# Moving the forget-gate columns of an encoder layer into seven-product form, and token-major work beside the recurrence heads

## The chip, the cores and the metric

One core of a Trainium2 chip runs the whole program. The metric is the device time of one launch in microseconds (us), a median of several runs. TensorE (PE in the profile) multiplies matrices, VectorE (DVE), ScalarE (ACT) and GpSimd (POOL) work elementwise, and SyncE (SP) issues every DMA of this kernel from one queue, in order. Each engine executes its own list of instructions in the order that was fixed when the program was built.

## The reference

One encoder layer with 1024 positions and 1024 channels, in float32. The parts that matter here:

```
h = rms_norm(x);  z = h @ W_in          # q | f_fwd | f_bwd | i | out-gate | u | v | gate_a | gate_b
f = lb + (1-lb)*sigmoid(zf);  k = (1-lb)*sigmoid(-zf)       # forget gates and keys, two directions
o = scan_forward(q, k_f, v, f_f) + scan_backward(q, k_b, v, f_b)   # 8 heads of 128
A = rms_norm(o) * silu(zg)
u = gelu(zu);  v = layer_norm(gelu(zv))                      # the gated branch, 512 channels each
sg[g] = w_s[g] @ v[chunk, g] + b_s[g]                        # per chunk of 128 positions and group of 64
B = u * sg
mix = (sigmoid(gate_a)*(A @ W_a) + sigmoid(gate_b)*(B @ W_b)) @ W_out
x = x + rms_norm(mix);  x = x + rms_norm(SwiGLU(rms_norm(x)))
```

## The kernel before

**Products.** A float32 operand is split into a high and a low part (`split_into`, L114 on ScalarE and L115 on VectorE), and a product is three passes of matmuls (`mm3`, L133): 24 matmuls of 512 columns for one 128 x 512 block over 1024 channels. `Seven` (its matmuls are L278) computes a 2 x 2 block product with seven products of 12 matmuls in place of eight, so 84 matmuls where `mm3` takes 96. Its weight sums cost VectorE and ScalarE extra work.

**Stages.** After the start come the token-major groups (`tm_group`: positions on the partitions, 8 tiles x 24 matmuls each): the branch's v, the first half of the values i, the branch's u, the second half of the values. Between them lie the 8 spatial gating matmuls (L450), the transposes of B, and B @ W_b (`branch_b`: 8 column blocks x 2 x 12 matmuls). Then come 14 jobs of `Seven` for the columns gate_b, half of gate_a, the output gate zg and q; each result goes to DRAM (`m0_d`, `sig_d`, `zg_d`, `q_d`), and gate_b is multiplied there with B @ W_b.

**Heads.** `scores(h)` first multiplies q with keys (L613, operands `q,ks`), and then goes through seven levels (m = 1, 2, ... 64). A level is two groups of four 128 x 128 matmuls `ps_sc<-QA,X` (L624); VectorE updates `QA` (L633) and `X` (L636) for the next level, merges the result into `SC` (L646 copy_predicated up to m = 16, ScalarE L643 above), GpSimd makes `Y` (L660), VectorE halves `F` (L666). So every level waits for VectorE's update from the level ahead of it. `outputs(h)` transposes keys (L683), forms states (`S`: matmuls L688, VectorE L694), sums the output (`ps_o`, L712), normalises it on ScalarE (L715, L719; the root on GpSimd L101), transposes it (`ps_tr<-ident,on`, L722), and writes it to `at_d` (`on`, L724). In the program's order `proj` of head h+1 stands between `scores(h)` and `outputs(h)`: it computes the forward and the backward gate columns of one head, 2 x 2 x 24 = 96 matmuls `ps_mm<-hT..,whl` by `mm3`. In the last head `gate_a(0)` and `gate_a(1)` compute the other four blocks of gate_a, 8 x 24 matmuls. These matmuls, which no level waits for, are called fill below. After the heads come `merge` (A @ W_a, `ps_mm<-A,whl`), the output projection and the feed-forward part.

**Order.** The program is written under `tile.TileContext(nc, schedule_with_timeline_sim=True)`: the builder decides where each engine's instructions stand; tiles in pools (`bufs`) set what has to be free first.

Of the kernel before, what the change touches and what calls it, by code (L numbers as in the profile page):

```python
# [9 lines left out]
F32 = mybir.dt.float32  # L10
F32R = mybir.dt.float32r
# [11 lines left out]
H = 8  # L23
# [12 lines left out]
def kernel(ctx: ExitStack, tc: tile.TileContext, a: dict, out: bass.AP):  # L36
# [42 lines left out]
    v_d = dram.tile([H, P, NT, P], F32, name="v_d")  # L79
    m0_d = dram.tile([KD, P, T], F32, name="m0_d")  # L80
# [3 lines left out]
    bw_d = dram.tile([KD, P, T], F32, name="bw_d")  # L84
# [288 lines left out]
    def ev_i(half):  # L373
        def f(t, ps):
            s = t2(p0v, "vs", 4)
# [5 lines left out]
    def ev_u(t, ps):  # L381
        nc.scalar.activation(u[:, t], ps, AF.Gelu)

    def load_tm(gi, kk):
        pool = p0w if (4 * gi + kk) % 6 < 4 else whlp
        return load_split(a["w_tm"][gi, kk], [2, NH], nc.gpsimd if kk % 2 else nc.vector, pool, rawp)
# [26 lines left out]
    w = [load_tm(0, 0), load_tm(0, 1)]  # L413
# [3 lines left out]
    w += [load_tm(0, 2), load_tm(0, 3)]  # L417
# [5 lines left out]
    vn, u = [sgu.tile([P, NT, SGW], F32, name=name, tag="uv", bufs=2) for name in ("vn", "u")]  # L423
# [11 lines left out]
    w = [load_tm(1, kk) for kk in range(4)]  # L435
# [5 lines left out]
    close(c_x)  # L441
    tm_group(w, ev_i(0), layer_norm)
    close(c_t)
    w = [load_tm(2, kk) for kk in range(4)]
    tm_group(w, ev_u)
    for g in range(SGG):
        ps = ps_any()
        es = slice(g * SGE, (g + 1) * SGE)
        pv = ps.rearrange("p (c e) -> p c e", e=SGE)
        nc.tensor.matmul(pv, lhsT=wst[:, g, :], rhs=vn[:, :, es], start=True, stop=True)  # L450
        nc.vector.scalar_tensor_tensor(out=u[:, :, es], in0=pv, scalar=sgb[:, g:g + 1], in1=u[:, :, es],
                                       op0=ALU.add, op1=ALU.mult)
    c_b, p1b = phase("p1b", side="right")
    bT = [pair(p1b, f"bT{n}", None) for n in range(2)]
    for t in range(NT):
        tp = ps_tile(("tr", "o")[t % 2])
        for i in range(4):
            nc.tensor.transpose(tp[:, i * P:(i + 1) * P], u[:, t, i * P:(i + 1) * P], ident)
        ts = slice(t % 4 * P, (t % 4 + 1) * P)
        split_into(bT[t // 4][0][:, :, ts], bT[t // 4][1][:, :, ts], tp.rearrange("p (k t) -> p k t", k=4))  # L460
    w = [load_tm(3, kk) for kk in range(4)]
    tm_group(w, ev_i(1))
    close(c_w, c_v)

# [8 lines left out]
    def branch_b(j):  # L473
        raw = rawp.tile([P, KD, P], F32, name="raw", tag="raw")
        nc.sync.dma_start(raw[:, 0:4], a["w_b"][j])
        wb = whlp.tile([P, 2, KD, P], F32R, name="whl", tag="whl")[:, :, 0:4]
        split_into(wb[:, 0], wb[:, 1], raw[:, 0:4])
        for n in range(2):
            ps = ps_any()
            mm3(ps, lambda p, k: wb[:, p, k, :], lambda p, k: bT[n][p][:, k, :], 4)  # L480
            s = t2(p1t, "o", 2)
            nc.scalar.activation(s, ps, AF.Copy)
            nc.sync.dma_start(bw_d[j, :, n * NH:(n + 1) * NH], s)

    branch_b(0)
    branch_b(1)
# [10 lines left out]
    for k in range(4):  # L497
# [11 lines left out]
    for j in range(2, KD):  # L509
        branch_b(j)  # L510
    close(c_b)
# [36 lines left out]
    close(c_e, c_w, c_r, c_t, c_T)  # L548
# [3 lines left out]
    c_t, t1 = phase("s1t", 2)  # L552

# [7 lines left out]
    def proj(s, h, kinds):  # L561

        for kind in kinds:
            if kind == "q":
                s.q = hg.tile([P, T], F32, name="q", bufs=2)
                nc.sync.dma_start(s.q, q_d[h])  # L570
# [523 lines left out]
```

## Time and profile before

| what | value |
|---|---|
| median of 3 runs | 1968.68 us (1968.6 to 1969.14) |
| the profiled execution's own time | 1966.99 us |
| its span in the trace | 1965.2 us |
| mean granted TensorE clock | 0.997 |
| PE busy | 1910.8 us, 97% of the span |
| DVE busy | 1120.0 us, 57% |
| ACT busy | 757.2 us, 39% |
| POOL busy | 206.7 us, 11% |

The span is 1.8 us shorter than the execution's own time, which lies 1.7 us under the median. A stage is read from the row of its window: how long it is, and how much of it each engine was busy.

### The profile page before, as it was taken

To read this page: it belongs to the slowest core of one execution; us is meant where nothing else is said; L and a number is where in the kernel's file an instruction comes from. 1 tells how busy PE (TensorE), PEld (TensorE's weight loads), DVE (VectorE), ACT (ScalarE), POOL (GpSimd) and SP (SyncE) were. 2 spreads that over 40 slices of the span, in tenths; PEclk is the share of its full clock that TensorE was granted. 3 is DMA by queue.
4 is the path that set the end of the run, shared out by engine and by line. 5 is a ranking of instruction groups with operands and counts; after the bars stand their busy time and mean duration, and the time that the engine had idled before them with its cause. 6 is when DMAs were issued, how large, how long until landed. Compare 5 with 4: busy or idle time off the path is not lost.

```text
span 1965.2 us, 24005 instructions
## 1 busy us (share of the span) xinstructions
PE 1910.8 (97%) x9264; PEld 1596.0 (81%) x9264; DVE 1120.0 (57%) x1712; ACT 757.2 (39%) x1424; POOL 206.7 (11%) x153
## 2 busy tenths in 40 slices
PE   7999999999999999999989998999999999999999
PEld 6887888888887888888877887888888888888887
DVE  7402385544348777777665468855554537545743
ACT  6312254343354545545441356433333324112321
POOL 2600000000012222222112100000000000001000
PEclk9999999999999999999999999999999999999999
DMA  7220245323231221212336333232222106315222
GB/s 292 93 88 27 87 172 170 130 105 110 86 123 33 70 71 63 66 55 68 126 106 208 107 99 103 97 112 78 89 76 86 65 33 209 108 65 163 92 102 79
DMA packets 82690, 201.86 MB, mean 103 GB/s; under 512 B 8720, under 2 KB 18064, under 8 KB 82576
## 3 DMA queue, kind: packets, MB, share of 16 engines
q1 hardware_dynamic: 82576, 200.33, 30.2%
q8 instruction: 73, 1.20, 0.3%
q14 instruction: 41, 0.34, 0.0%
HBM read 147.35 MB, written 52.95 MB: 102 GB/s over the span
## 4 chain that ended last, share of the span: by engine, by line
PE 90%; DVE 4%; ACT 2%; DMA 2%; POOL 1%; issue 1%; SPq 0%; DVEq 0%; POOLq 0%; ACTq 0%
PE ps_mm L133 29%; PE ps_mm L278 20%; PE ps_sc L133 11%; PE ps_sc L278 10%; PE ps_st L133 6%; PE ps_sc L624 4%; PE ps_o L278 2%; PE ps_o L712 2%; PE ps_tr L278 2%; PE ps_st L278 1%; DVE QA L633 1%; POOL Y L660 1%; PE ps_st L688 1%; ACT SC L643 0%; DMA raw<-in_w_gate_dram 0%
## 5 line engine op out<-in xcount | busy, mean ns | idle before, releaser
L278 PE MATMUL ps_mm<-T,w 128*128 128x512 f32 x1296 | 309.6, 389 | 0.0
L278 PEld LDWEIGHTS ps_mm<-T,w 128*128 128x128 f32 x1296 | 243.2, 188 | 50.7 <-ACT u L228 0.2
L115 DVE TENSOR_TENSOR whl<-raw,whl 128x1024 fp32r<-128x1024 f32 (+1 forms) x70 | 89.6, 1282 | 142.7 <-ACT whl L114 142.6
L660 POOL TENSOR_TENSOR Y<-X,F 128x512 f32<-128x512 f32 x56 | 92.4, 1651 | 696.1 <-DVE F L599 392.4
L624 PE MATMUL ps_sc<-QA,X 128*128 128x128 f32 x896 | 126.4, 288 | 16.9 <-DVE QA L633 16.9
L115 DVE TENSOR_TENSOR w<-sums,w 128x1024 fp32r<-128x1024 f32 x72 | 88.0, 1223 | 94.2 <-ACT w L114 94.2
L624 PEld LDWEIGHTS ps_sc<-QA,X 128*128 128x128 f32 x896 | 116.1, 192 | 26.1 <-DVE QA L633 19.0
L133 PE MATMUL ps_mm<-whl,act 128*128 128x512 f32 x528 | 134.1, 389 | 0.0
L114 ACT ACTIVATE whl<-raw 128x1024 fp32r<-128x1024 f32 (+1 forms) x78 | 79.1, 1017 | 120.2 <-PE ps_sc L133 52.4
L633 DVE TENSOR_TENSOR QA<-QA,F 128x512 f32<-128x512 f32 x112 | 91.8, 828 | 49.2 <-PE ps_sc L624 48.1
L133 PE MATMUL ps_mm<-hTb,whl 128*128 128x512 f32 x480 | 118.6, 396 | 0.0
L133 PEld LDWEIGHTS ps_mm<-whl,act 128*128 128x128 f32 x528 | 99.1, 188 | 20.7
L133 PE MATMUL ps_mm<-hTa,whl 128*128 128x512 f32 x480 | 115.1, 392 | 0.0
L114 ACT ACTIVATE w<-sums 128x1024 fp32r<-128x1024 f32 x72 | 75.9, 1055 | 99.9 <-PE ps_sc L278 76.9
L278 PE MATMUL ps_sc<-T,w 128*128 128x512 f32 x432 | 107.5, 389 | 0.0
L133 PEld LDWEIGHTS ps_mm<-hTa,whl 128*128 128x128 f32 x480 | 89.4, 188 | 18.1
L133 PEld LDWEIGHTS ps_mm<-hTb,whl 128*128 128x128 f32 x480 | 88.2, 188 | 16.8
L278 PEld LDWEIGHTS ps_sc<-T,w 128*128 128x128 f32 x432 | 81.1, 188 | 16.9
L133 PE MATMUL ps_sc<-whl,act 128*128 128x512 f32 x354 | 91.0, 390 | 0.3 <-ACT acc L953 0.3
L133 PEld LDWEIGHTS ps_sc<-whl,act 128*128 128x128 f32 x354 | 66.3, 188 | 14.3 <-ACT acc L953 0.7
L115 POOL TENSOR_TENSOR wpg<-raw,wpg 128x1024 fp32r<-128x1024 f32 x4 | 9.6, 2403 | 598.3 <-ACT wpg L114 593.6
L278 PE MATMUL ps_mm<-B,wA 128*128 128x512 f32 x264 | 67.3, 399 | 1.7 <-ACT wA L114 1.7
(309 smaller groups left out, 3574.2 us busy)
## 6 DMA issues: line engine op xcount, KB each, us to landing
raw<-in_w_fm_dram SPq DMA_DIRECT2D x52, 512.0 KB, 3.6
raw<-in_w_gate_dram SPq DMA_DIRECT2D x22, 512.0 KB, 3.4
raw<-in_w_up_dram SPq DMA_DIRECT2D x22, 512.0 KB, 3.9
act_d<-s SPq DMA_DIRECT2D x22, 512.0 KB, 2.8
raw<-in_w_down_dram SPq DMA_DIRECT2D x22, 512.0 KB, 4.4
raw<-act_d SPq DMA_DIRECT2D x22, 512.0 KB, 4.2
raw<-in_w_tm_dram SPq DMA_DIRECT2D x16, 512.0 KB, 4.1
pr_d<-vs SPq DMA_DIRECT2D x16, 256.0 KB, 5.9
```

What stands on the lines that cost most here:

```text
L114: nc.scalar.activation(hi, src, AF.Copy)
L115: (eng or nc.vector).tensor_tensor(out=lo, in0=src, in1=hi.bitcast(F32), op=ALU.subtract)
L133: nc.tensor.matmul(ps, lhsT=lhs(lp, k), rhs=rhs(rp, k), start=(i == 0), stop=(i == n - 1))
L278: nc.tensor.matmul(ps, lhsT=lhs(lp, k), rhs=rhs(rp, k), start=(first and i == 0), stop=(i == n - 1), skip_group_check=True)
L624: nc.tensor.matmul(sp[:, i * P:(i + 1) * P], lhsT=X[:, c * P:(c + 1) * P], rhs=view(QA, c * P, [[2 * m, cb], [T + m, 2], [1, m]]), start=T ...
L633: nc.vector.tensor_tensor(out=view(QA, o, qd), in0=view(QA, o, qd), in1=view(F, of + 1, [[nb - 1, 2], [2, nb // 4], [0, m]]), op=ALU.mult)
L660: nc.gpsimd.tensor_tensor(out=view(Y, m, mid), in0=view(X, m, mid), in1=view(F, 0, [[4, nb // 4], [nb + 3, 2], [0, m]]), op=ALU.mult)
L688: nc.tensor.matmul(up[:, i * P:(i + 1) * P], lhsT=kt[:, i], rhs=v[:, c], start=True, stop=True)
L712: nc.tensor.matmul(op[:, i * P:(i + 1) * P], lhsT=l, rhs=r, start=(j == 0), stop=(j == len(terms) - 1))
```

## The change

1. `proj` is gone from the heads. The forget gates and keys of head h become a job ("fb", h) of `Seven`, with the forward columns as one block and the backward columns as the other. Eight such jobs stand among the column jobs (22 instead of 14). `gates` evaluates them and writes `F`, `X` and `Y` to DRAM (`f_d`, `xk_d`, `yk_d`); `load_head` reads them back ahead of each head. The temporaries `o` get 4 buffers instead of 2.
2. Three stages that stood ahead of the columns now stand beside the heads, where `proj` was: the second half of the values (heads 0 and 1), the gated branch u times `sg_d`, written to `ub_d` (heads 2 and 3), its transposes and B @ W_b (heads 4 and 5). gate_b is only written (`gb_d`) in the columns and multiplied in `branch_b`.
3. gate_a(0) moves to head 6, gate_a(1) stays in head 7. The finished heads' outputs are read back (`load_A`, `split_A`) there, two heads at a time. `v`, `zg`, `q` and `X` have one buffer each instead of two, and `load_values` stands behind `outputs` of the head before.
4. The T operands of `Seven` (`sums`) are made beside the second token-major group, and the layer norm of v inside the first.

```
-    tm_group(w, ev_u)
     for g in range(SGG):
         nc.tensor.matmul(pv, lhsT=wst[:, g, :], rhs=vn[:, :, es], start=True, stop=True)
-        nc.vector.scalar_tensor_tensor(out=u[:, :, es], in0=pv, scalar=sgb[:, g:g + 1], in1=u[:, :, es],
+        nc.scalar.activation(vn[:, :, es], pv, AF.Identity, bias=sgb[:, g:g + 1])
+    for t in range(NT // 2):
+        nc.sync.dma_start(sg_d[t], vn[:, 2 * t:2 * t + 2])
...
-    tm_group(w, ev_i(1))
...
-    branch_b(0)
-    branch_b(1)
...
-    for j in range(2, KD):
-        branch_b(j)
...
+    def gates(h, blocks):
+        for n in range(2):
+            ns = slice(n * NH, (n + 1) * NH)
+            keys = [t2(p1t, "o", 4) for _ in range(2)]
+            for d in range(2):
+                c = blocks[2 * d + n]
+                om = oml[:, d, h:h + 1]
+                cv = c.rearrange("p (t h) -> p t h", h=2)
+                for par in range(2):
+                    k = keys[par != d].rearrange("p (t h) -> p t h", h=2)[:, :, par]
+                    nc.scalar.activation(k, cv[:, :, par], AF.Sigmoid, scale=-1.0)
+                    nc.vector.tensor_scalar(out=k, in0=k, scalar1=om, scalar2=None, op0=ALU.mult)
+                Fd = t2(p1t, "o", 4) if 2 * d + n == 2 else c
+                nc.scalar.activation(Fd, c, AF.Sigmoid)
+                nc.vector.tensor_scalar(out=Fd, in0=Fd, scalar1=om, scalar2=lbt[:, d, h:h + 1], op0=ALU.mult, op1=ALU.add)
+                nc.vector.tensor_scalar(out=Fd, in0=Fd, scalar1=TINY, scalar2=None, op0=ALU.max)
+                nc.sync.dma_start(f_d[h, :, 1 - d, ns], Fd)
+            for k, k_d in zip(keys, (xk_d, yk_d)):
+                nc.sync.dma_start(k_d[h, :, ns], k)
...
-    jobs = [(kind, j) for kind, n in (("gb", KD), ("ga", NGA), ("zg", H), ("q", H)) for j in range(0, n, 2)]
+    jobs = [(kind, j) for kind, n in (("gb", KD), ("ga", NGA)) for j in range(0, n, 2)]
+    jobs = [job for h in range(6) for job in (("fb", h), jobs[h])] + [("fb", 6), ("fb", 7)]
+    jobs += [(kind, j) for kind in ("q", "zg") for j in range(0, H, 2)]
...
-            w = load_split(a["w_fm"][{"f": 8, "b": 16}[kind] + h], [KD, P], None, whlp, rawp)
-            for n in range(2):
-                mm3(ps, lambda p, k: w[:, p, k, :], fm_rhs(hT[n]), KD)
...
+    def load_head(s, h):
+        s.F = hg.tile([P, 2, T], F32, name="F")
+        nc.sync.dma_start(s.F, f_d[h])
...
-            proj(nxt, h + 1, "qfbg")
-        if h == H - 1:
+            load_head(nxt, h + 1)
+        if h < 2:
+            values(range(4 * h, 4 * h + 4))
...
+        elif h < 4:
+            branch(range(4 * (h - 2), 4 * (h - 1)))
+        elif h == 4:
+            bT = [pair(tmw, f"bT{n}", "tmw") for n in range(2)]
+            transpose_b(bT)
+            branch_b(bT, (0,))
+        elif h == 5:
+            branch_b(bT, (2, 4, 6))
+        elif h == 6:
             gate_a(0)
             A0 = new_fm("A0")
-            load_A(0, A0, range(H - 1), 5)
+            load_A(range(6))
+            for i in range(3):
+                split_A(0, A0, i)
+        else:
+            load_A([6])
             gate_a(1)
             A1 = new_fm("A1")
+            split_A(0, A0, 3)
...
         outputs(h, cur)
+        if h + 1 < H:
+            load_values(nxt, h + 1)
```

Three places show how the instructions moved. The first is TensorE's list (PE) in the middle of a late head, around the output sums of the head before (`ps_o`). Before, this piece of head 5 reads:

```order
2281 L712 MATMUL ps_o<-S,QA 128x128
2282 L624 MATMUL ps_sc<-QA,X 128x128 x2
2283 L133 MATMUL ps_mm<-hTb_150,whl 128x512
2284 L133 MATMUL ps_mm<-hTb_152,whl 128x512
2285 L133 MATMUL ps_mm<-hTb_150,whl 128x512
2286 L133 MATMUL ps_mm<-hTa_145,whl 128x512
2287 L133 MATMUL ps_mm<-hTa_147,whl 128x512
```

In the changed kernel the last four heads read like this (`A` is the normed output of earlier heads, `kt` transposed keys, `st` the state's sum):

```order
2509 L603 MATMUL ps_sc<-QA,X 128x128 x4
2510 L667 MATMUL ps_st<-v,kt 128x128 x3
2511 L603 MATMUL ps_sc<-QA,X 128x128 x12
2512 L667 MATMUL ps_st<-v,kt 128x128 x3
2513 L603 MATMUL ps_sc<-QA,X 128x128 x8
2514 L691 MATMUL ps_o<-S,QA 128x128
```

Where 24 or more fill matmuls stood between two levels, the levels now follow each other with only the short matmuls of `outputs` between them. The rows of the list say how the fill is spread. Before, 115 fill matmuls stand ahead of head 0's `q,ks` (counted from the last matmul of the columns), and between the `q,ks` of one head and the next 128, 96, 96, 96, 96, 96 and 143. In the changed kernel 79 stand ahead of head 0's, and then 213, 110, 153, 161, 43, 12 and 0 between them.

The second place is TensorE's list behind the last level of the last head (`X`, `Y` and `kt` are keys, `ps_st` the states' sums). Before, the transposes of both halves of head 6's outputs (rows 2709 and 2726) stand ahead of head 7's last levels:

```order
2726 L722 MATMUL ps_tr<-ident,on 128x128 x4
2727 L624 MATMUL ps_sc<-QA,X 128x128 x8
2728 L133 MATMUL ps_mm<-A_7479,whl 128x512 x2
2729 L133 MATMUL ps_mm<-A_7481,whl 128x512
2730 L133 MATMUL ps_mm<-A_7479,whl 128x512
2731 L133 MATMUL ps_mm<-A_7481,whl 128x512
2732 L133 MATMUL ps_mm<-A_7479,whl 128x512
2733 L624 MATMUL ps_sc<-QA,X 128x128 x8
```

In the changed kernel the last level of head 7 is row 2613, and behind it both halves of head 6's outputs follow (`ps_o`, and their transposes in rows 2626 and 2635), and then, as the last matmuls ahead of head 7's own outputs:

```order
2649 L667 MATMUL ps_st<-v,kt 128x128 x3
2650 L138 MATMUL ps_mm<-A_7353,whl 128x512 x2
2651 L138 MATMUL ps_mm<-A_7355,whl 128x512
2652 L138 MATMUL ps_mm<-A_7353,whl 128x512
2653 L138 MATMUL ps_mm<-A_7355,whl 128x512
2654 L138 MATMUL ps_mm<-A_7353,whl 128x512
2655 L667 MATMUL ps_sc<-v,kt 128x128 x3
2656 L691 MATMUL ps_sc<-v,SC 128x128
```

Rows 2650 to 2654 are six matmuls of `merge` that read the part of A in which head 6 lies, so they need its outputs written, read back and split. 42 matmuls `ps_sc<-A,whl` of `merge` (rows 2671 to 2703) stand in two parts of 21 ahead of the two transposes of head 7's outputs (rows 2687 and 2704), where before both transposes stand in one row with no matmul of `merge` between them.

The third place is VectorE's list (DVE) inside the column jobs. Before, it holds the sums, splits and adds of `Seven` there, and in the gate_b jobs four products with B @ W_b:

```order
302 L266 TENSOR_TENSOR p_3203<-ps_mm,p_3203 128x512
303 L268 TENSOR_TENSOR u_3217<-ps_sc,u_3217 128x512
304 L115 TENSOR_TENSOR w_3410<-sums,w_3410 128x1024
305 L203 TENSOR_TENSOR sums<-raw_3427 128x512
306 L204 TENSOR_TENSOR sums<-sums,raw_3422 128x512
```

In the changed kernel the gate arithmetic of a job of the new kind stands among them (`o`, `u` and `p` hold keys and gates, `oml` and `lbt` the bounds):

```order
187 L531 TENSOR_SCALAR o<-o,oml 128x256 x2
188 L534 TENSOR_SCALAR o<-o,oml,lbt 128x512
189 L531 TENSOR_SCALAR o<-o,oml 128x256 x2
190 L535 TENSOR_SCALAR o<-o 128x512
191 L120 TENSOR_TENSOR w_1571<-raw_1452,w_1571 128x512
192 L271 TENSOR_TENSOR p_1482<-ps_mm,p_1482 128x512
```

A whole job of the new kind adds eight such rows of 128x256 and eight of 128x512 to VectorE's list.

## Rows read from the trace of the kernel before

**Rows 1.** The page: PE's busy time, and the chain that ended last by engine.

```profile
PE 1910.8 (97%) x9264; PEld 1596.0 (81%) x9264; DVE 1120.0 (57%) x1712; ACT 757.2 (39%) x1424; POOL 206.7 (11%) x153
...
PE 90%; DVE 4%; ACT 2%; DMA 2%; POOL 1%; issue 1%; SPq 0%; DVEq 0%; POOLq 0%; ACTq 0%
```

**Rows 2.** Windows of stages: length, busy times, granted clock, DMA share, GB/s.

```profile
core 0: us, PE busy (x) PEld busy (x) DVE busy (x) ACT busy (x) POOL busy (x), PEclk, DMA share, GB/s
...
282.00:540.00 258.00, 258.00 (x1140) 213.64 (x1139) 125.29 (x162) 102.48 (x148) 0.00 (x0) 1.00 0.36 123
...
692.90:745.80 52.90, 49.06 (x321) 44.00 (x320) 40.53 (x71) 27.59 (x71) 14.01 (x9) 1.00 0.20 65
```

**Rows 3.** Timeline of PE: start, duration, work, where stages begin.

```profile
131.51 1.79 PE L133 MATMUL ps_mm<-whl,hTa 128*128 128x512 f32 x7
...
176.00 1.02 PE L450 MATMUL ps_mm<-vn,wst 128*128 128x512 f32 x2
...
182.87 0.27 PE L458 MATMUL ps_tr<-ident,u 128*128 128x128 f32 x1
...
275.95 0.63 PE L278 MATMUL ps_mm<-hTa,wA 128*128 128x512 f32 x2
...
547.30 0.84 PE L133 MATMUL ps_mm<-hTa,whl 128*128 128x512 f32 x3
...
583.76 1.49 PE L624 MATMUL ps_sc<-QA,X 128*128 128x128 f32 x8
```

**Rows 4.** Timeline of PE within one column job.

```profile
292.75 2.88 PE L278 MATMUL ps_mm<-T,w 128*128 128x512 f32 x12
295.47 2.88 PE L278 MATMUL ps_sc<-T,w 128*128 128x512 f32 x12
```

**Rows 5.** Groups of instructions in the heads: busy us, mean ns | idle before.

```profile
L633 DVE TENSOR_TENSOR QA<-QA,F 128x512 f32<-128x512 f32 x112 | 91.8, 828 | 49.2 <-PE ps_sc L624 48.1
...
L646 DVE COPY_PREDICATED SC<-masks,ps_sc 128x512 f32<-128x512 uint8 x80 | 58.5, 733 | 0.0
L636 DVE TENSOR_TENSOR X<-X,F 128x256 f32<-128x256 f32 x110 | 57.9, 558 | 0.2
...
L115 DVE TENSOR_TENSOR whl<-raw,whl 128x1024 fp32r<-128x1024 f32 x22 | 26.8, 1218 | 12.1 <-ACT whl L114 12.0
...
L591 ACT ACTIVATE sk<-ps_mm 128x512 f32<-128x512 f32 x27 | 16.1, 597 | 7.3 <-PE ps_mm L133 7.3
...
L599 DVE TENSOR_SCALAR F<-F 128x512 f32<-128x512 f32 x28 | 11.2, 419 | 1.4 <-ACT F L598 1.4
```

**Rows 6.** Windows in a head where the fill has run out.

```profile
719.00:741.00 22.00, 18.16 (x137) 16.71 (x136) 19.06 (x37) 14.00 (x35) 8.93 (x5) 1.00 0.25 85
```

**Rows 7.** Timeline of PE in that stretch, idle time ahead in brackets.

```profile
722.96 2.05 PE L624 MATMUL ps_sc<-QA,X 128*128 128x128 f32 x16 [0.68 <-DVE QA L633]
...
726.05 2.02 PE L624 MATMUL ps_sc<-QA,X 128*128 128x128 f32 x16 [0.17 <-DVE QA L633]
...
732.69 0.33 PE L683 MATMUL ps_tr<-ident,X 128*128 128x128 f32 x1 [1.28 <-ACT kt L685]
```

**Rows 8.** Timeline of PE behind the last level of the last head.

```profile
1004.63 1.06 PE L688 MATMUL ps_st<-v,kt 128*128 128x128 f32 x8
...
1014.34 0.61 PE L712 MATMUL ps_o<-S,QA 128*128 128x128 f32 x4
1017.86 1.10 PE L722 MATMUL ps_tr<-ident,on 128*128 128x128 f32 x4 [2.92 <-ACT on L719]
1019.90 1.09 PE L722 MATMUL ps_tr<-ident,on 128*128 128x128 f32 x4 [0.94 <-DVE on L724]
1020.64 2.69 PE L133 MATMUL ps_mm<-A,whl 128*128 128x512 f32 x6
...
1037.58 4.60 PE L133 MATMUL ps_mm<-A,whl 128*128 128x512 f32 x19 [1.74 <-DVE whl L115]
```

**Rows 9.** DMA issues: KB each, median us from issue to landing.

```profile
at_d<-on SPq DMA_DIRECT2D x14, 256.0 KB, 2.1
xr<-at_d SPq DMA_DIRECT2D x12, 256.0 KB, 3.9
```

**Rows 10.** Windows of the first matmuls behind that wait: granted clock in column PEclk.

```profile
1018.00:1021.00 3.00, 2.06 (x9) 1.54 (x9) 1.30 (x2) 2.25 (x8) 0.44 (x1) 0.75 0.00 0
1021.00:1024.00 3.00, 2.93 (x9) 1.83 (x8) 2.84 (x6) 2.10 (x5) 0.00 (x0) 0.68 0.14 35
```

More of the change, by code (lines that the diff above doesn't have):

```diff
@@ L371, in layer_norm, with ev_i @@
         nc.gpsimd.tensor_tensor(out=vn[:, t], in0=c, in1=lnb, op=ALU.add)
-    def ev_i(half):
+    def ev_i(half, pool, role):
         def f(t, ps):
-            s = t2(p0v, "vs", 4)
+            s = t2(pool, role, 4 if half == 0 else 2)
             nc.scalar.activation(s, ps, AF.Copy)
@@ L379, in ev_i, with load_tm @@
         return f
[L381 to L386, printed above, removed]
+    def load_tm(gi, kk, pool, tag="whl"):
+        return load_split(a["w_tm"][gi, kk], [2, NH], nc.gpsimd if kk % 2 else nc.vector, pool, rawp, tag)
     def tm_group(w, per_tile, ahead=None):
@@ L412 @@
     norm_x(0)
-    w = [load_tm(0, 0), load_tm(0, 1)]
+    w = [load_tm(0, kk, p0w2) for kk in (0, 1)]
     for t in range(4):
@@ L416 @@
     load_pw(0, 1)
-    w += [load_tm(0, 2), load_tm(0, 3)]
+    w += [load_tm(0, kk, p0w) for kk in (2, 3)]
     load_x(2)
@@ L422 @@
             ple_product(e, t)
-    vn, u = [sgu.tile([P, NT, SGW], F32, name=name, tag="uv", bufs=2) for name in ("vn", "u")]
+    close(c_pw)
     def x_ahead(t):
@@ L434 @@
     tm_group(w, ev_v, x_ahead)
-    w = [load_tm(1, kk) for kk in range(4)]
+    w = [load_tm(1, kk, whlp if kk < 2 else p0w) for kk in range(4)]
     nc.sync.dma_start(wst, a["wst"])
@@ L495, in sum_of, with sums @@
             acc = out
-    for k in range(4):
+    def sums(k):
         sa, sb = [st1.sum_tile().rearrange("p a k c -> p a (k c)") for _ in range(2)]
@@ L508 @@
         split_into(T4[0][:, k], T4[1][:, k], sb[:, 1])
-    for j in range(2, KD):
-        branch_b(j)
-    close(c_b)
+    tm_group(w, ev_i(0, p0v, "vs"), lambda t: sums(t // 2) if t % 2 else None)
+    for g in range(SGG):
+        ps = ps_any()
+        es = slice(g * SGE, (g + 1) * SGE)
+        pv = ps.rearrange("p (c e) -> p c e", e=SGE)
+        nc.tensor.matmul(pv, lhsT=wst[:, g, :], rhs=vn[:, :, es], start=True, stop=True)
+        nc.scalar.activation(vn[:, :, es], pv, AF.Identity, bias=sgb[:, g:g + 1])
+    for t in range(NT // 2):
+        nc.sync.dma_start(sg_d[t], vn[:, 2 * t:2 * t + 2])
+    close(c_t, c_w, c_v, c_sgu)
     c_r, p1r = phase("p1r", 2)
@@ L755, in gate_a, with load_A, split_A @@
             nc.sync.dma_start(sig_d[j, :, n * NH:(n + 1) * NH], sg)
+    rawA = {}
+    def load_A(hs):
+        for h in hs:
+            if h % 2 == 0:
+                rawA[h // 2] = tmw.tile([P, 2, T], F32, name="rawA", tag="tmw")
+            nc.sync.dma_start(rawA[h // 2][:, h % 2], at_d[h])
+    def split_A(n, A, i):
+        w = 1 if 2 * i + 1 == H - 1 else 2
+        k = 2 * i % 4
+        split_into(A[0][i // 2][:, k:k + w, :], A[1][i // 2][:, k:k + w, :], rawA[i][:, 0:w, n * NH:(n + 1) * NH])
     cur = Head()
-    proj(cur, 0, "qfbg")
+    load_head(cur, 0)
+    tw[3] = [load_tm(3, kk, whlp if kk < 2 else tmw, "whl" if kk < 2 else "tmw") for kk in range(4)]
+    load_values(cur, 0)
     for h in range(H):
```

182 lines of the change are left out of this document (93 added, 89 removed).

## The prediction

> **What bounds the kernel now.** I read the page first. PE is busy 97% of the span, and the chain that ended last runs through PE for 90% of its length [rows 1]; VectorE, next in that chain, has 4%. So a matmul taken away should be worth its spacing on PE, wherever PE has no idle time. The windows by stage say where that holds. In the columns PE is busy for all of 258 us, VectorE for 125.3, ScalarE for 102.5 [rows 2]. In a steady head PE is busy 49.1 of 52.9 us and VectorE 40.5 [rows 2]: here the reader is to see a second engine not far behind the first. The groups of instructions say what VectorE does there: `QA`, `X` and the copy_predicated, 828, 558 and 733 ns each [rows 5]. Then I read the timeline of a head where its 96 matmuls of fill have run out. There PE waits for VectorE's `QA` ahead of every level (0.68 and 0.17 us), levels stand 3.1 us apart, and in 22.0 us VectorE is busy 19.06 and PE 18.16 [rows 6, 7]. Fill therefore does two things: it is PE's work, and it covers the heads' chain through VectorE. Last come the tail behind the heads [rows 8] and DRAM round trips [rows 9].
>
> **What is removed and added.** The spacing of matmuls of 512 columns is 2.72 us per 12 in the columns, 0.2267 each [rows 4]; in token-major work it is 44.49 us from 131.51 to 176.00 for 8 x 24, 0.2317 each [rows 3]. `proj` had 8 x 96 = 768 matmuls, the new jobs have 8 x 84 = 672: 96 fewer, 96 x 0.2267 = 21.8 us of PE. This is the whole saving; everything else only moves.
>
> *Ahead of the columns.* From 131.51 to 275.95 PE did the u group, the gating matmuls, transposes, the second half of the values, and B @ W_b, 144.4 us [rows 3]. Only the gating matmuls stay (176.00 to 182.87, 6.9 us), so 137.6 us leave. The eight new jobs bring 672 x 0.2267 = 152.3 us. The columns end 14.8 us later, if nothing but PE bounds the new jobs. The `sums` that stood beside B @ W_b lie beside the second token-major group, and layer norm inside the first; I price both moves at nothing, since PE has no idle time in the stages they leave and enter, and a late T operand would show as idle time at the first job.
>
> *The new jobs.* A job takes PE 84 x 0.2267 = 19.05 us. The 258 us hold 13.5 jobs, so VectorE has 9.3 us and ScalarE 7.6 us in one. `gates` adds to VectorE eight 128x512 rows at 0.42 [rows 5] and eight of 128x256, each between half and all of that: 5.0 to 6.7 us, 14.3 to 16.0 of 19.05. ScalarE gets four sigmoids of 0.60 [rows 5] in place of four results, and eight of 128x256 at 0.3 to 0.6: 10 to 12.4 us. Both stay under PE, so 0; if the queues in order or the four `o` buffers held a job back as far as VectorE's whole sum lay on PE's path for one quarter of it, it would be about 4 us in each of the 8 jobs. I keep 0 to 20 us for the range.
>
> *Start of the heads.* From 547.30 to the end of the first level (583.76 + 0.9 for its last four matmuls, their drain left out) was 37.3 us [rows 3], with 147 fill matmuls in the list. The new list has 122 there: 122 x 0.2325 + 3.6 for the short ones = 31.9. That is -5.4.
>
> *The levels.* From 584.65 to the last level's end at 1004.63 [rows 3, 8] is 420.0 us. The new fill is spread 213, 110, 153, 161 over the first four stretches and 43, 12, 0 over the rest. For the first four heads I add the rows of the list between two levels for PE and for VectorE and take the larger each time: PE alone gives 223.5 us, the larger of the two 239.3. The same sum over the eight heads before gives 388.5 where the trace has 420.0, four us per head too little, since waits inside a level are left out; with ample fill I add half of that, 2 each, and take 247. For the last four, PE has only 109 us of work. At the mean durations of the groups a steady head's VectorE list comes to 45.3 us where it was busy 40.5 (records overlap); the last four heads' lists come to 163.1, so 163.1 x 40.5 / 45.3 = 146 us busy. At the share that VectorE reached where fill had run out, 19.06 / 22.0 [rows 6], they take 168 us; 146 if VectorE never waits. I take 165, between the two and near the row. Levels: 412, -8. Bounds: 223.5 + 146 = 370 and 255 + 180 = 435.
>
> *The tail.* From 1004.63 to the first matmul behind the last transpose (1020.64) is 16.0 us [rows 8]. Now all of head 6's outputs follow the last level too. The rows up to the last transpose are 27.4 us of PE's work, 9.5 of it being 42 matmuls of `merge` that are thereby done. The waits: each half of head 6's outputs has the norm chain before its transpose, 2.92 us in [rows 8]; and the six matmuls that read head 6's part of A wait for the norm's end, a write of 2.1 us, a read of about 3.9 [rows 9] and a split, some 9 us, of which 5.5 are covered by rows between. That is 9.3 us, if nothing else covers them; I take 6.6, so 34.0: +18.0, and -9.5 for the `merge` matmuls. Behind them, the wait of 1.74 us for VectorE's split of a weight [rows 8] may go: -1.7.
>
> **The sum.** 14.8 - 5.4 - 8 + 18 - 9.5 - 1.7 = +8.2 us. On the profiled execution's own time, 1966.99, that is 1975.2; the median of the runs lies 1.7 higher, so about **1976.5 us**. In words: 21.8 us of PE's work go, and about 30 us of idle time on PE come in heads 4 to 7 and behind them, because the work that filled them stands in the first four heads.
>
> **The rivals.** (1) *The saving comes through whole.* If the last four heads and the tail cost PE no more idle time than the heads had (3.8 us each [rows 2]), the time is 1968.7 - 21.8 = 1947. For it: PE has 90% of the chain. Against it: the late lists hold 109 us of matmuls against 146 of VectorE. It needs VectorE's share there near 1 and the four heads at 146, and the tail's waits covered; half of that gives 1958 to 1962. Chance 0.27 for ending under 1964.7.
>
> (2) *No change.* The first four heads run at PE's 223.5 instead of 247, or the tail's waits are covered, but not all: 1965 to 1972.6. Chance 0.2.
>
> (3) *The clock falls in the thin stretches.* The one long wait of PE at the end of the heads, 2.92 us [rows 8], is followed by windows whose granted clock is 0.75 and 0.68 [rows 10], so much of them at the 1.2 GHz level. The stretch without fill, with waits up to 1.28 us [rows 7], keeps 1.00 [rows 6]. The late heads have 109 us of matmuls in 165, thinner than any stretch of before. At half the clock for a quarter of these 109 us, 27 us of matmuls take 27 us more, part of it in idle time: +10 to +20, 1986 to 1997. It decides from waits as long as the 2.92 on.
>
> The Trainium skill, in "TensorE: Matmul & The Clock Gate", section "A second HAM failure mode: psum-queue depth-cycling", says that frequent small idle gaps between groups of matmuls suffice to make the clock swing. By that rule the late heads would fall under rival 3, 1986 to 1997; the stretch with waits of 0.17 to 1.28 us shows 1.00 [rows 6, 7] and does not bear it out, so its chance stays at 0.15.
>
> (4) *The new jobs are held by VectorE, ScalarE or the four `o` buffers.* From 19.05 us of VectorE's work in a job on, the columns grow; 2 us in each of eight jobs is 16 us, 1992. Against it: 16.0 is the upper sum. Likewise a late `load_head` (1 MB of `F` from DRAM, one buffer) behind `load_values`, which waits for the outputs of the head before. Chance 0.08.
>
> **How the numbers follow.** My forecast, 1972.6 to 1986, has 0.30; with rivals 1 to 4 (0.27, 0.20, 0.15, 0.08) that is 1. The measurement tells from no change about 0.2%, 3.9 us. Faster 0.27, same 0.20, slower 0.53. The range reaches 1952 (about 0.1 of rival 1 left out) and 1995 (0.1 of rivals 3 and 4). The likeliest case's own range is 1968 to 1986.
>
> **What would show it.** Right: columns without idle on PE and ending near 562; the first four heads near 250 us with PE almost full; heads 4 to 7 with PE waiting for `QA`, VectorE above 85%, levels 3 us apart; more than 30 us between the last level and the last transpose. Wrong: heads 4 to 7 in under 150 us; a granted clock under 0.95 there (rival 3); idle time of PE in the columns ended by VectorE, ScalarE or `o` (rival 4); a tail of 20 us.

## The result, and the profile after

The changed kernel takes 1998.5 us (median of 4 runs, 1992.1 to 2001.4) against 1968.7: 1.0147 times as long, with a 95% interval of 1.0122 to 1.0171. It is slower, as forecast, but by 30 us where 8 were expected, and outside the range. A second group of runs gave 1.0165 (1.0151 to 1.0179). The profiled execution took 1999.0 us, with a span of 1997.2, 32.0 longer than before.

The page of the changed kernel, in the lines that answer to [rows 1]:

```profile
PE 1913.6 (96%) x9168; PEld 1603.6 (80%) x9168; DVE 1200.5 (60%) x1870; ACT 737.7 (37%) x1383; POOL 203.7 (10%) x153
...
PE 87%; DVE 7%; DMA 3%; ACT 1%; issue 1%; POOL 0%; SPq 0%; DVEq 0%; ACTq 0%; POOLq 0%
```

PE has 96 matmuls fewer and is busy 2.8 us longer: part of its work ran slower. Its idle time, span less busy time, went from 54.4 to 83.6 us. The prediction's sum holds 30 us more of idle time and 21.8 us less of busy time; 29.2 more and 2.8 more came. VectorE's part of the chain rose from 4% to 7%. The timeline of PE, at the places of [rows 3] and [rows 8], says in which stage the time went:

```profile
563.69 17.46 PE L138 MATMUL ps_mm<-whl,hTa 128*128 128x512 f32 x75
...
594.79 1.49 PE L603 MATMUL ps_sc<-QA,X 128*128 128x128 f32 x8
...
835.75 1.95 PE L603 MATMUL ps_sc<-QA,X 128*128 128x128 f32 x16
...
1017.06 2.05 PE L603 MATMUL ps_sc<-QA,X 128*128 128x128 f32 x16
...
1062.24 0.60 PE L701 MATMUL ps_tr<-ident,on 128*128 128x128 f32 x4
1062.60 1.63 PE L138 MATMUL ps_mm<-A,whl 128*128 128x512 f32 x6
```

The columns end at 563.69, 16.4 us later than before; the first level of head 0 is done 32.0 us behind that (594.79 and 0.9 for its last four matmuls), where it took 37.3 before, so 5.3 are won back; 837.5 ends head 3's last level and 1018.9 head 7's, 423.2 us of levels against 420.0; the tail is 43.7 us against 16.0; what follows is 10.0 shorter (934.6 against 944.6). 16.4 - 5.3 + 3.2 + 27.7 - 10.0 = 32.0.

Windows, with the columns of [rows 2], from one product of q with keys to another: heads 0 to 3, heads 4 to 6, head 7, tail.

```profile
581.90:840.50 258.60, 249.31 (x1483) 220.77 (x1482) 175.22 (x291) 91.97 (x217) 51.13 (x37) 0.99 0.49 165
840.50:962.70 122.20, 95.51 (x650) 88.28 (x648) 106.47 (x181) 44.30 (x124) 33.26 (x25) 0.92 0.33 112
962.70:1019.10 56.40, 39.19 (x237) 36.01 (x237) 38.06 (x64) 18.80 (x52) 11.60 (x9) 0.82 0.12 38
1019.10:1062.60 43.50, 35.67 (x200) 30.92 (x198) 11.13 (x28) 13.52 (x57) 4.03 (x4) 0.84 0.33 109
```

The reader is to see three different things. With plenty of fill PE is nearly full. In heads 4 to 6 VectorE is busy 106.47 of 122.2 us, 87%, and PE waits for it. In head 7 VectorE is down to 38.06 of 56.4 and in the tail to a quarter, and the granted clock is 0.82 and 0.84. But the mean of head 7 hides two stages. Up to 990 VectorE mostly waits itself; from 990 to 1010 it is nearly full, with splits of `A` (L120) between the updates of the levels:

```profile
962.70:990.00 27.30, 18.08 (x94) 16.43 (x94) 11.83 (x20) 6.98 (x29) 5.09 (x4) 0.75 0.08 29
990.00:1010.00 20.00, 14.24 (x105) 12.67 (x103) 18.96 (x31) 8.90 (x13) 4.97 (x5) 1.00 0.21 67
...
981.15 2.29 DVE L585 TENSOR_TENSOR QA<-q,F 128x2048 f32<-128x2048 f32 x1 [2.77 <-PE ps_o L691]
...
1006.54 2.61 DVE L120 TENSOR_TENSOR A<-rawA,A 128x1024 fp32r<-128x1024 f32 x2
```

The timeline of PE shows what it waits for:

```profile
868.40 2.02 PE L603 MATMUL ps_sc<-QA,X 128*128 128x128 f32 x16 [3.02 <-DVE ov L104]
...
908.75 3.76 PE L603 MATMUL ps_sc<-QA,X 128*128 128x128 f32 x16 [3.57 <-DVE QA L612]
...
976.35 1.25 PE L701 MATMUL ps_tr<-ident,on 128*128 128x128 f32 x4 [2.92 <-ACT on L698]
...
983.55 2.04 PE L603 MATMUL ps_sc<-QA,X 128*128 128x128 f32 x8 [2.43 <-ACT on L694]
...
1012.23 3.76 PE L603 MATMUL ps_sc<-QA,X 128*128 128x128 f32 x16 [4.13 <-DVE QA L612]
...
1026.41 1.10 PE L701 MATMUL ps_tr<-ident,on 128*128 128x128 f32 x4 [2.93 <-ACT on L698]
...
1034.52 1.25 PE L701 MATMUL ps_tr<-ident,on 128*128 128x128 f32 x4 [2.93 <-ACT on L698]
```

The outputs of head 5 stand inside head 7's levels, and those of head 6 behind them. Three of the four halves bring a wait of 2.9 us for the norm, and no fill stands in these places. The 2.43 us at 983.55 are put down to ScalarE's squares of the fourth (head 5's second half), but end with VectorE's first `QA` of head 7 (L585, done at 983.44): `QA` has two buffers, so VectorE starts it only when head 5's output sums (`ps_o`) have read theirs. Sixteen records of a level take 3.76 us behind the waits of 3.57 and 4.13, and 1.95 at full clock (835.75 above). Not every long wait is followed by half clock: behind the 3.02 us at 868.40 they take 2.02.

In the tail the chain that ended last leaves PE for some 11 us. Behind the transposes of head 6's second half it goes through the norm's end, the write, the read and the split of head 6's outputs; PE's transposes and states of head 7, at half clock, lie beside it:

```profile
1027.51 4.10 PE ps_o L691 x22
...
1036.59 2.39 DMA at_d<-on
...
1039.04 4.99 DMA rawA<-at_d
...
1044.72 1.29 DVE A L120 x2
```

**A measure for the experiments.** The order's rows give PE's work at full clock: 0.2267 us a matmul of 512 columns (0.2317 token-major), 0.222 a 128 x 128 product, 0.111 a transpose. From head 0's `q,ks` to the first matmul behind the last transpose, the time less this work is what PE lost to waits and to the low clock:

| kernel | PE's work | time | lost |
|---|---|---|---|
| before | 393.5 | 447.3 | 54 |
| changed | 372.6 | 480.7 | 108 |
| e5, fill held back | 378.2 | 469.6 | 91 |
| e6, seven jobs, held | 399.3 | 459.5 | 60 |
| e11, six jobs, held | 421.0 | 474.6 | 54 |
| e7, five jobs, held | 440.8 | 492.9 | 52 |
| e12, four jobs, held | 461.9 | 509.4 | 48 |
| e4, four jobs, not held | 459.6 | 514.0 | 54 |

By window the changed kernel lost 19 us in heads 0 to 3 (239.5 of work in 258.6), 44 in heads 4 to 6 (78.2 in 122.2), 29 in head 7 (27.4 in 56.4) and 16 in the tail (27.5 in 43.5). Work went down by 21, the loss up by 54. Over the whole stretch PE was busy 415.34 us before and 419.68 in the changed kernel, so some 29 of the 54 us are idle time and 25 are work that took longer. That doesn't say what the low clock cost: where slow work lies beside a longer chain, full clock would only turn it into idle time.

```profile
573.36:1020.64 447.28, 415.34 (x2643) 370.29 (x2642) 333.61 (x575) 223.97 (x567) 105.92 (x71) 1.00 0.21 69
```

```profile
581.90:1062.60 480.70, 419.68 (x2562) 375.98 (x2560) 330.89 (x562) 168.59 (x449) 100.02 (x73) 0.94 0.39 132
```

### The profile page after: what moved, and what is told of

It reads as the page before. It is cut to its first block, busy times and chain, and to the rows that moved or that the text cites. A ratio compares the mean times of both kernels' runs of the same rounds, so it can differ in the third digit from the quotient of the medians.

```text
span 1997.2 us, 24233 instructions
## 1 busy us (share of the span) xinstructions
PE 1913.6 (96%) x9168; PEld 1603.6 (80%) x9168; DVE 1200.5 (60%) x1870; ACT 737.7 (37%) x1383; POOL 203.7 (10%) x153
## 4 chain that ended last, share of the span: by engine, by line
PE 87%; DVE 7%; DMA 3%; ACT 1%; issue 1%; POOL 0%; SPq 0%; DVEq 0%; ACTq 0%; POOLq 0%
PE ps_mm L283 24%; PE ps_mm L138 22%; PE ps_sc L283 12%; PE ps_sc L138 9%; PE ps_st L138 5%; PE ps_sc L603 4%; PE ps_o L283 2%; PE ps_tr L283 2%; PE ps_st L283 2%; DVE QA L612 2%; PE ps_o L691 2%; DVE X L615 1%; DMA m_d<-gb 1%; DVE SC L625 1%; PE ps_st L667 1%
## 5 line engine op out<-in xcount | busy, mean ns | idle before, releaser
L283 PE MATMUL ps_mm<-T,w 128*128 128x512 f32 x1584 | 378.5, 389 | 0.0
L283 PEld LDWEIGHTS ps_mm<-T,w 128*128 128x128 f32 x1584 | 297.3, 188 | 61.9 <-ACT u L233 0.2
L120 DVE TENSOR_TENSOR w<-sums,w 128x1024 fp32r<-128x1024 f32 x88 | 107.7, 1224 | 102.1 <-ACT w L119 102.1
L119 ACT ACTIVATE w<-sums 128x1024 fp32r<-128x1024 f32 x88 | 92.8, 1056 | 119.9 <-PE ps_sc L283 83.6
L283 PE MATMUL ps_sc<-T,w 128*128 128x512 f32 x528 | 131.7, 389 | 0.0
L119 ACT ACTIVATE whl<-raw 128x1024 fp32r<-128x1024 f32 x58 | 61.0, 1058 | 134.8 <-PE ps_sc L138 51.2
L120 DVE TENSOR_TENSOR whl<-raw,whl 128x1024 fp32r<-128x1024 f32 x50 | 69.1, 1386 | 45.6 <-ACT whl L119 45.6
L138 PE MATMUL ps_mm<-whl,hTb 128*128 128x512 f32 x312 | 75.8, 395 | 0.0
L271 DVE TENSOR_TENSOR p<-ps_mm,p 128x512 f32<-128x512 f32 x44 | 30.4, 691 | 70.6 <-PE ps_mm L283 70.6
L120 POOL TENSOR_TENSOR wpg<-raw,wpg 128x1024 fp32r<-128x1024 f32 x4 | 9.6, 2404 | 596.9 <-ACT wpg L119 596.9
L120 POOL TENSOR_TENSOR whl<-raw,whl 128x1024 fp32r<-128x1024 f32 x8 | 21.7, 2717 | 477.6 <-ACT whl L119 476.9
L138 PE MATMUL ps_mm<-whl,hTa 128*128 128x512 f32 x288 | 70.1, 397 | 0.0
```

The source lines that it names most:

```text
L119: nc.scalar.activation(hi, src, AF.Copy)
L120: (eng or nc.vector).tensor_tensor(out=lo, in0=src, in1=hi.bitcast(F32), op=ALU.subtract)
L138: nc.tensor.matmul(ps, lhsT=lhs(lp, k), rhs=rhs(rp, k), start=(i == 0), stop=(i == n - 1))
L271: nc.vector.tensor_tensor(out=c22, in0=X, in1=c22, op=ALU.add)
L283: nc.tensor.matmul(ps, lhsT=lhs(lp, k), rhs=rhs(rp, k), start=(first and i == 0), stop=(i == n - 1), skip_group_check=True)
```

## The experiments

**e1: PE kept at work in heads 4 to 7.** Matmuls whose results nothing reads:

```
             def level(g):
                 sp = ps_tile("sc")
+                if h >= 4:
+                    for i in range(4):
+                        nc.tensor.matmul(sp[:, i * P:(i + 1) * P], lhsT=ks[:, i * P:(i + 1) * P], rhs=q[:, i * P:(i + 1) * P], start=True, stop=True)
...
             tp = ps_tile("tr")
+            if h >= 4:
+                for i in range(4):
+                    for j in range(3):
+                        nc.tensor.matmul(tp[:, i * P:(i + 1) * P], lhsT=SC[:, 4 * g + i], rhs=v[:, 4 * g + i], start=(j == 0), stop=(j == 2))
```

> Changed kernel with matmuls that nothing reads added in heads 4 to 7: four ahead of every half of a level (224 in all, 50 us of TensorE's work at 0.222 us) and twelve ahead of each half head's output transposes (96, 21 us). The order of the other work stays as in the changed kernel. Theory A (the late heads are bound by VectorE, and the lower clock is a side effect that mostly falls into idle time): granted clock from 880 to 1050 us rises above 0.97, the last four heads stay at 160 to 170 us, only the tail behind the last level gets shorter, by 4 to 8 us; total 0 to -10 us against the changed kernel. Theory B (the lower clock itself is the price): late heads and tail together get 20 us or more shorter, about 1975. If the added work is on the path, it is slower, up to +30.

2006.7 us (1.0190, 1.0173 to 1.0208). The windows from head 4's `q,ks` on:

```profile
844.60:1045.30 200.70, 189.19 (x1536) 182.93 (x1536) 144.20 (x251) 68.20 (x201) 44.99 (x35) 0.99 0.26 87
1045.30:1074.00 28.70, 26.86 (x189) 24.25 (x187) 7.54 (x21) 8.33 (x32) 2.01 (x2) 1.00 0.32 110
```

With the idle time filled, the clock is back. But the 71 us of added work filled PE (189 of 200.7), the levels got 22 us longer and the tail 15 shorter, and in this list head 6's outputs stand ahead of the last level again. What the clock costs can't be read from this.

**e2: only ahead of the output transposes of heads 6 and 7.** The second piece above with `if h >= 6`.

> Changed kernel with twelve matmuls that nothing reads ahead of each half's output transposes in heads 6 and 7 only (48, 10.7 us of work, put where TensorE waits 2.9 us for the norm). Theory A: the wait stays, and the sums of outputs behind it run at full clock, so the tail of 43.7 us becomes 37 to 40, total -4 to -7 us. Theory B: -10 us or more. If the fallen clock comes from the idle time in the late heads and not from these waits: no change.

1999.8 us (1.0163, 1.0138 to 1.0188): no change. The tail's clock rose from 0.84 to 0.96, and its length from 43.5 to 46.3 us. Head 7's transposes already have 21 matmuls of `merge` ahead of each, so half of the added work filled no wait. The matmuls were badly placed.

**e8 and e10: ahead of those of heads 5 and 6.** The same piece with `if h in (5, 6)`. The builder put only half of it where it was meant: the matmuls of each head's first half run earlier, between levels, and the wait of 2.9 us ahead of these transposes stays; those of the second half stand where PE waited for head 7's first `QA` and for the norm. It also moved a few of the other instructions in PE's list, levels of head 7 among them.

> Changed kernel with twelve matmuls that nothing reads ahead of each half's output transposes of heads 5 and 6 only (48, 10.7 us at 0.222), where TensorE waits 2.4 to 2.9 us for the norm each time and the granted clock fell to 0.66 to 0.69; the order of the rest stays. If the fallen clock is 8 us of the tail and some of head 7's stretch: these four places run at full clock, -5 to -12 us. If the waits alone matter: 0, or slower by what sticks out of the waits, 1 to 3 us.

> The kernel with matmuls that nothing reads ahead of the output transposes of heads 5 and 6, in more rounds: in the first profile the granted clock of head 7's stretch and of the tail rose from 0.82 and 0.84 to 0.93 and 1.00 and these two got 8.5 us shorter. If the fallen clock is a price on the path: 4 to 9 us below the changed kernel of the same group. If it falls into idle time: within 3 us of it.

> The changed kernel itself, timed on the chip of the other runs of this group: 1992 to 2001, for the comparison with the run with warmed outputs.

e8: 1995.8 us (1.0136, 1.0112 to 1.0161). e10: 1997.5 us (1.0137, 1.0121 to 1.0154) beside the changed kernel e9 with 2002.1 us (1.0165, 1.0151 to 1.0179). So 10.7 us of useless work made the kernel some 4.6 us faster beside e9; the two intervals still touch, and e8 is only 2.7 us under the first group of the changed kernel, within the noise. Head 7 and the tail in e8, and in e10:

```profile
962.60:1014.40 51.80, 39.13 (x280) 36.20 (x279) 37.66 (x63) 18.04 (x50) 11.29 (x9) 0.93 0.13 42
1014.40:1054.00 39.60, 32.70 (x222) 28.44 (x221) 10.86 (x28) 13.62 (x57) 4.03 (x4) 1.00 0.36 120
```

```profile
965.90:1019.60 53.70, 41.35 (x279) 38.61 (x278) 38.06 (x63) 18.01 (x50) 11.04 (x9) 0.87 0.12 40
1019.60:1061.60 42.00, 36.11 (x225) 31.86 (x223) 10.87 (x28) 13.59 (x57) 4.03 (x4) 0.92 0.34 113
```

The waits of head 6's two halves in e8's tail:

```profile
1021.74 1.11 PE L706 MATMUL ps_tr<-ident,on 128*128 128x128 f32 x4 [2.93 <-ACT on L698]
...
1028.22 1.10 PE L706 MATMUL ps_tr<-ident,on 128*128 128x128 f32 x4 [0.24 <-ACT on L698]
```

In e8 the clock is 0.93 and 1.00 for 0.82 and 0.84, and the two stretches are 4.6 and 3.9 us shorter; in e10 it is 0.87 and 0.92, and they are 4.2 us shorter together. Some of the low clock lay on the path here. The 4 to 8 us can't be put down to it alone, as the list changed too: e2, without added matmuls ahead of head 5's transposes, also has a shorter head 7 (52.1 us). Seen on the chain itself, the sums of head 6's second half (`ps_o`) take 4.10 us in the changed kernel and 2.47 in e8.

**e3: less work for VectorE.** Heads 4 to 7 skip the copy_predicated of the levels up to m = 16.

```
+                if h >= 4:
+                    return
                 nc.vector.copy_predicated(
```

> Changed kernel in which heads 4 to 7 leave out the copy_predicated of the levels up to m = 16 (40 instructions of 0.73 us, 29 us of VectorE's work), so these heads' scores miss those levels. Theory A (VectorE bounds the last four heads): they shorten by 20 to 29 us, from 166 to about 140; total about 1972. Theory B (TensorE's clock or the length of the chain bounds them): under 8 us. Theory C (loads behind single buffers bound them): under 5 us.

1986.4 us (1.0080, 1.0063 to 1.0097), 12 less than the changed kernel, and from head 4's `q,ks` to the last level 166.5 us instead of 178.5. PE's list is nearly the same: a few level groups, state matmuls and a transpose stand elsewhere. 12 of 29 us: VectorE is on the path of the late heads for some of its work only. All three theories missed. What makes up the rest isn't shown; PE's other waits and the way back and forth between the two engines are the candidates.

**e5: the same work, spread.** Before each head's fill, three tiles in the ring of `ps_mm` that need this head's keys:

```
         scores(h, cur)
+        if h in (1, 2, 3, 4, 5, 6, 7):
+            for i in range(3):
+                dm = ps_tile("mm")
+                nc.tensor.matmul(dm[:, 0:P], lhsT=cur.ks[:, 0:P], rhs=cur.ks[:, 0:P], start=True, stop=True)
```

> Changed kernel with the same work, but the work beside each of heads 1 to 7 is held back: three one-matmul tiles that read this head's key sum stand ahead of it in the ring of buffers of its matmul results, so it cannot start before its head does (21 small matmuls more). The fill between the products of q with keys becomes 96, 96, 96, 48, 67, 119, 134 matmuls of 512 columns in place of 213, 110, 153, 161, 43, 12, 0. Theory A (idle time of TensorE in the last four heads because their cover was used up early): those heads are covered again, the idle time goes, total 1955 to 1975. Theory V (VectorE's total work in the heads is the bound, however the fill is spread): within 8 us of the changed kernel, 1990 to 2006.

1984.3 us (1.0077, 1.0059 to 1.0094), 14 less than the changed kernel, where theory A had 24 to 44. Its windows: heads 0 to 4, 5 and 6, 7, tail.

```profile
580.70:835.90 255.20, 229.40 (x1453) 205.54 (x1452) 196.80 (x335) 90.71 (x234) 64.69 (x46) 0.95 0.38 129
835.90:955.70 119.80, 111.29 (x690) 99.49 (x688) 86.35 (x143) 43.98 (x106) 22.96 (x17) 0.97 0.52 183
955.70:1008.40 52.70, 44.19 (x279) 39.35 (x278) 37.51 (x63) 21.37 (x56) 11.04 (x8) 0.97 0.22 74
1008.40:1050.30 41.90, 33.41 (x194) 28.68 (x192) 9.75 (x25) 13.47 (x57) 4.03 (x4) 0.88 0.34 113
```

In the trace the fill from one product of q with keys to the next is 96, 96, 96, 48, 67, 100 and 132. The loss moved instead of going: 46 us in heads 0 to 4 now (209 of work in 255.2), and the tail is nearly as long as in the changed kernel. A head with 96 matmuls of fill still takes 53 us, as before, one with 48 takes 47. So it was not only the spread: eight heads with this amount of fill hold too little of PE's work for their pace. From head 0's `q,ks` to the last level e5 takes 427.6 us, and the kernel before 431.3; what makes e5 slower than before lies mostly in its tail, 41.9 us against 16.0 (9.5 of it are matmuls of `merge` that stand there now).

**e6, e11, e7, e12, e4: some gates computed beside the heads again.** For heads from N on, 96 direct matmuls of fill beside the head ahead (in e6, e11, e7 and e12 with fill held back in heads 1 to 6, 1 to 6, 1 to 3, and 1 and 2), N = 7, 6, 5, 4; e4 is N = 4 without holding:

```
-    jobs = [job for h in range(6) for job in (("fb", h), jobs[h])] + [("fb", 6), ("fb", 7)]
+    jobs = [job for h in range(8) for job in ([("fb", h)] if h < N else []) + jobs[h:h + 1] * (h < 6)]
...
-            load_head(nxt, h + 1)
+            (load_head if h + 1 < N else direct_head)(nxt, h + 1)
```

`direct_head` is the `proj` of before for one head, with `q` loaded first. With N = 4 the branch of head 3 stands ahead of it.

> Changed kernel in which the gates of heads 4 to 7 are again computed directly beside the heads (4 x 96 matmuls as fill) and only heads 0 to 3 have their seven-product job ahead; everything else is as in the changed kernel. TensorE gets 48 matmuls more, 10.9 us. Theory A (what was lost is the cover of the late heads): columns end 76 us earlier, the late heads are covered again, tail near 20 us; total 1940 to 1960. Theory C (the loads, single buffers and trips through DRAM are what costs): no better than the changed kernel, about 2000 or more, since these stay and the work is 10.9 us more.

> As the run that holds the fill back, for heads 1 to 6, and head 7's gates are computed directly beside head 6 (96 matmuls of fill) in place of its seven-product job: 12 matmuls of 512 columns more than the changed kernel, 2.7 us. In the list head 6's outputs then stand ahead of head 7's last level again. Theory A: a shorter tail (under 30 us in place of 43.7), so 10 to 20 us below the run with held fill alone: 1940 to 1960. If the tail's length came from its own norm waits and not from head 6's outputs standing there: no better than that run.

> Gates of heads 5 to 7 direct beside heads 4 to 6, fill of heads 1 to 3 held back; 36 matmuls more than the changed kernel, 8.2 us. The fill is 96, 96, 96, 72, 72, 192, 240. Theory A: every head has cover, tail as before (16 to 20 us), so the saving that is left, 13.6 us, comes through together with some of the idle time of before: 1935 to 1955. Theory C (loads and single buffers): not below before, 1968 or more.

> Gates of heads 6 and 7 direct beside heads 5 and 6, the fill of heads 1 to 6 held back: 24 matmuls more than the changed kernel, 5.4 us. The fill is 96, 96, 96, 48, 72, 120, 240. Theory A: between the run with five heads in seven-product form (1952) and that with seven (1959), 1950 to 1960.

> Gates of heads 4 to 7 direct beside heads 3 to 6, the fill of heads 1 and 2 held back: 48 matmuls more than the changed kernel, 10.9 us. The fill is 96, 97, 167, 96, 72, 192, 240. Theory A (a head's pace stays near its 46 us of VectorE and waits until it has some 96 matmuls, and from there on every matmul costs its 0.2267 us): 2.7 us per head above the run with five, 1952 to 1960; against the run with four heads without holding (1956), -5 to 0, as the stretch without any fill goes.

| kernel | us | ratio to before, 95% |
|---|---|---|
| e4, N = 4, not held | 1955.7 | 0.9934 (0.9919 to 0.9949) |
| e6, N = 7 | 1958.5 | 0.9949 (0.9931 to 0.9966) |
| e11, N = 6 | 1956.4 | 0.9934 (0.9920 to 0.9947) |
| e7, N = 5 | 1952.5 | 0.9920 (0.9897 to 0.9942) |
| e12, N = 4 | 1951.2 | 0.9902 (0.9889 to 0.9916) |

All five beat both kernels, with 12 to 48 matmuls more than the changed one. (In the traces of e7 and e12 the last figure of the fill is 194, not 240.) The first step is the large one: from e5 to e6, 96 matmuls beside head 6 in place of 84 in the columns are 2.7 us more work, and the time falls by 26. In the list head 6's outputs then stand ahead of head 7's last level again. Which of the two counts, the work beside head 6 or the order, this step doesn't separate. Head 7 and the tail of e6, and of e7:

```profile
948.00:999.70 51.70, 48.87 (x309) 44.45 (x309) 33.60 (x58) 20.53 (x53) 8.60 (x7) 0.97 0.30 100
999.70:1021.40 21.70, 21.24 (x138) 18.77 (x137) 7.84 (x21) 8.24 (x33) 2.01 (x2) 1.00 0.24 92
```

```profile
923.00:990.90 67.90, 67.00 (x402) 59.15 (x402) 44.84 (x73) 29.66 (x65) 11.63 (x8) 1.00 0.33 109
990.90:1013.90 23.00, 21.84 (x139) 18.83 (x138) 7.81 (x21) 8.33 (x32) 2.02 (x2) 1.00 0.43 149
```

The tail is 21.7 and 23.0 us in place of 41.9, at full clock and with PE nearly always busy. So it is in all profiles: where head 6's outputs stand behind the last level (the changed kernel, e2, e3, e5, e8, e9, e10) the tail takes 39.6 to 46.3 us, where they stand ahead of it (e1, e4, e6, e7, e11, e12) 21.7 to 28.7. e12's gain, some 19 us, is more than its 10.9 us of matmuls fewer than before; 6 us less lost in the table are most of the rest. All these kernels keep the single buffers for `v`, `zg`, `q` and `X` and the trips through DRAM of the changed kernel (for seven, six, five or four heads' gates), so theory C, that the loads cost the time, falls as the main cause; that they cost nothing isn't shown, since no kernel with two buffers was tried.

## Why the prediction was right or wrong

**The direction and half of the mechanism held:** PE lost its cover in the late heads, and that outweighs 21.8 us of matmuls. The idle time came as forecast, 29 us for 30. What failed is the sum's step that PE's work, idle time aside, takes the same time as before: it was to be busy 21.8 us less and was busy 2.8 us more. **The columns** were to end 14.8 us later; 16.4, with no idle time of PE between 150 and 560 us, so the jobs' gate arithmetic was hidden, and that part of rival 4 is out. Its other part, a late `load_head`, shows as 10.2 us of VectorE's time in heads 0 to 3, waiting for keys, where PE had fill; from 840 on no wait of PE or VectorE is put down to a DMA. In other profiles of the same columns they ended at 560.3 to 564.1, so 1.6 us is within their spread. **The start of the heads**, 31.9, took 32.0; its 0.2325 us a matmul stands in no row, and the 37.3 us of [rows 3] less 3.6 give 0.229, so 31.6. **Heads 0 to 3**, 247 by the prediction, took 241.8. **Behind the tail**, -11.2 was expected and -10.0 measured.

Two terms were mis-sized by it. **The last four heads**, 165 us, took 181.4 (837.5 to 1018.9). VectorE's 146 us of work were right (106.5 + 38.1), and so was its share of 87% in heads 4 to 6. The step that failed is the use of that share [rows 6], from a stretch of short waits at full clock, for head 7 as well: there VectorE is busy 67%. Up to 990 head 5's outputs stand in head 7's stretch, with waits of 2.92 us for the norm and 2.43 us for head 7's first `QA`, and a clock of 0.75; behind it VectorE is full, but with splits of `A` besides the levels' updates, and PE waits 4.13 us. **The tail**, 34.0 us, took 43.7. PE's work there was priced at full clock, 27.4 us, and took 35.7; its waits were 7.7 us where 6.6 were taken. That doesn't make the low clock worth 8 us: much of the slow work lies beside the write, read and split of head 6's outputs, where PE would have waited otherwise, and e8's tail at clock 1.00 still takes 39.6. So about 4 of the 9.7 us can be the clock's. In e8's tail the waits (6.9 us) and the 12 added matmuls that stand in one of them (2.7) come to 9.6 us: that is near the 9.3 that the prediction had before it took 6.6. 1.6 - 5.2 + 16.4 + 9.7 + 1.2 = 23.7, and with the 8.2 forecast 32.

**Rival 3** was given 0.15 and is part of the truth: the clock was 0.92, 0.82 and 0.84 in the last three windows. The sum put it at nothing because the stretch of [rows 6] had kept 1.00. Its price on the path stays open: head 7 and the tail got 4 (e10) to 8 us (e8) shorter with more of the clock back, and for heads 4 to 6 no run gives the clock back without other changes. Rival 3's 10 to 20 us are neither shown nor ruled out. It should have been a term of the likeliest case, since [rows 8] and [rows 10] had it: a wait of 2.92 us, and half clock behind it, and the new list has the norm's wait three times without fill (2.92, 2.93 and 2.93 us). The Trainium skill ("TensorE: Matmul & The Clock Gate", section "A second HAM failure mode: psum-queue depth-cycling") ties such swings to frequent small gaps between groups of matmuls. This trace agrees with the swings and shows longer gaps with them: half clock came behind waits of 2.4 to 4.1 us, though not behind each (3.02 at 868.40, 2.93 in e8's tail), and the stretch with waits up to 1.28 us kept 1.00.

**Rivals 1 and 2**, the whole saving and no change, did not come about in this order of work. How much of the 44 us lost in heads 4 to 6 is VectorE's work, how much the clock and how much the length of the way PE to VectorE to PE stays open: e3 shows 12 us for 29 of VectorE's work.

## What to carry to other kernels

Work that nothing waits for is also cover: before taking it out of a loop whose pace another engine sets, count what is left for each pass, at the end of the loop above all, where the outputs of the last passes pile up behind each other. The tail alone grew from 16.0 to 43.7 us, 9.5 of it work brought forward, and fell to 22 to 29 where the outputs of the last head but one stood ahead of the last level again. Cheaper work ahead of the loop paid here only as long as the last heads kept their direct matmuls (four to seven of eight jobs moved: 0.5 to 1% faster; all eight: 1.5% slower). A share of busy time from one stretch holds for another only if the same things stand in it.

## What the runs showed of the hardware

Matmuls that nothing reads can bring the clock back: 48 of them, 10.7 us, raised the granted clock of the tail from 0.84 to 1.00 in e8 and to 0.92 in e10, and e10 was 4.6 us faster than e9 (intervals that touch). Where other work already stood in the wait, as in e2, nothing was gained.

Half clock need not lie on the path: from 1035.6 to 1044.7 PE's matmuls ran at half clock (0.51 granted) beside a write of 2.39 us and a read of 4.99 us that the chain waited for. And a wait of about the same length was followed by half clock in one place (2.93 us at 1026.41) and not in another (3.02 us at 868.40; 2.93 us in e8's tail).
